# SSD decay mask and per-sequence operands: 128-column ScalarE pieces in place of wide VectorE and GpSimd instructions

## The chip, the cores and the metric

One core of one Trainium2 chip runs the kernel. The metric is the device time of one execution in microseconds (us).

## The reference, cut to what matters

The kernel is one inference step of a hybrid decoder layer for 1024 prompt tokens and 8 sample sequences of 8 tokens (1088 tokens): a modulated norm, one wide input projection, three groups of dilated attention, a Mamba-2 (SSD) branch, and an output projection. The change lies in the SSD branch. For one head the reference computes, with chunks of 128 tokens:

```python
# cs: cumulative sum of dt*A within a chunk; xdt = x * dt
L   = exp(cs_i - cs_j)  for i >= j, else 0          # decay inside a chunk
y  += (C_i . B_j) * L[i, j] * xdt_j                  # masked, chunk by chunk
state_c = state_(c-1) * exp(cs_end) + sum_j B_j * exp(cs_end - cs_j) * xdt_j
# sample tokens: state_b' = state_b * exp(cs_end_b) + sum over the 8 tokens of sequence b
```

The masked decay is made from relu(cs_j - cs_i), then exp of its negative, then a product with the causally masked C.B (`CB`). The states of the 8 sample sequences need, for each sequence b, the 64 sample rows multiplied by a 0/1 column that is 1 on the rows of b (`bmask`).

## The kernel before, in words

fp32 products are done on TensorE (PE) as three matmuls of a high and a low part: hi*hi, hi*lo, lo*hi (`mm3`, lines 196, 197, 198). Before a weight tile is used, ScalarE (ACT) rounds it to its high part `whi` (line 189) and VectorE (DVE) subtracts to get the low part `wlo` (line 190).

The stages follow each other: start to about 100 us, attention to about 780 us, SSD from about 780 to 1560 us, output projection to the end. In the SSD stage `run(jobs)` does projection jobs, each in three chunks of 368, 368 and 352 columns with 24 matmuls a chunk. A job's results leave PSUM (3 banks for these `pj` tiles) by an evacuation: of a conv job by ACT into `raw` (lines 858, 860), then a causal convolution of width 4 (ACT line 873, three times DVE line 875), a tanh (ACT line 877) and the products of lines 880 and 882 (DVE) that finish `xc`; of a z job by tanh (ACT line 891) and a product that reads the same bank again (DVE line 892), which frees the bank; of a gate job by ACT (`sg`, line 457).

Beside them runs a side generator: per head group of 4 tiles, `side()` transposes B, multiplies C.B into `CB`, and calls `x_tile` for the tiles xt = 4*gr to 4*gr+3, 16 in all, two heads each. The order of TensorE's queue is written out by hand: the generator yields, with a planned number of ns, and its matmuls are put between the k steps of the projection at that point. For every other engine a scheduler (the tile framework) decides the order of the instructions from the program; each engine then works its queue strictly in that order, and waits at the head of it.

What `x_tile` does, by lines of the kernel before:

- Line 973: a DMA on SyncE's (SP) queue broadcasts two rows of `cs` into `csb` (128 x 2 x 1088). `csb` has one buffer, so it starts after the last `yd` matmul of the tile before.
- Lines 977 and 980 (DVE): tok - csb, in one instruction of 128x2048 for the prompt and one of 128x128 for the sample. Then per head: relu (ACT line 983) and exp(-x) (ACT line 984), 128x1088 each, and the product with `CB` (DVE line 985).
- After the conv job of this tile is done (`xc`), PE transposes it to tokens (`tt`, line 209), DVE makes `xdt` (line 1003), GpSimd (POOL) `xde` (line 1008), DVE `xd` (line 1011), ACT its high part `xdh` (line 1013) and DVE the rest (line 1014). Line 1016, twice: POOL multiplies `xdh` and `xd`, repeated 8 times, by `bmask`, into `xdm` (128x1024 each).
- `stt` matmuls; ACT copies the first chunk into `sta` (line 1029), and DVE chains 14 steps over the other seven chunks (line 1033). `yo` matmuls read `sta` (14 of them, in two PSUM banks), then `ys` (ACT line 1044), `u` (DVE lines 1055, 1060), the `sts` matmuls that read `xdm`, and later the `yd` matmuls that read `csb`; then `u` is finished (line 1090), squared on ACT (lines 1093, 1096) and added into `sq` on POOL.

By what stands next to a tile in the program there are four kinds. In tiles 2, 6, 10 the conv of the same tile runs while `csb` is made. Tiles 1, 5, 9, 13 and tiles 3, 7, 11, 15 have a gate or other evacuation between. Tiles 0, 4, 8, 12 open a head group, and the conv of the next group's B is near.

Of the kernel before, what the change touches and what calls it, by code (L numbers as in the profile page):

```python
# [11 lines left out]
AF = mybir.ActivationFunctionType  # L12
OP = mybir.AluOpType
# [4 lines left out]
T = 1024  # L18
NB = 8
NS = 8  # L20
TS = NB * NS
TT = T + TS
# [4 lines left out]
CH = 128  # L27
# [82 lines left out]
def trunk(ctx: ExitStack, tc: tile.TileContext, I, O):  # L110
    nc = tc.nc
    V, S, G, PE, SP = nc.vector, nc.scalar, nc.gpsimd, nc.tensor, nc.sync
# [34 lines left out]
    def P(name):  # L147
        a, n = PACK[name]
        return pack[:, a:a + n]
# [228 lines left out]
    tok = const.tile([128, 9, 96], F32, name="tok")  # L378
# [448 lines left out]
    with ExitStack() as bctx:  # L827
# [98 lines left out]
        def side():  # L926
            for gr in range(4):
# [24 lines left out]
                for xt in range(4 * gr, 4 * gr + 4):  # L952
                    yield from x_tile(gr, xt, Bk, Bs, CB, CT, CS, sq)
                    order.passed.add(("x", xt))
# [15 lines left out]
        def x_tile(gr, xt, Bk, Bs, CB, CT, CS, sq):  # L970
            h0 = 2 * xt
            csb = b1.tile([128, 2, TT], F32, tag="csb", name="csb")
            SP.dma_start(out=csb, in_=bass.AP(tensor=cs_d.tensor, offset=cs_d[0, h0].offset,
                                              ap=[[0, 128], [TT, 2], [1, TT]]))
            mt = [csb[:, h, :] for h in range(2)]

            V.tensor_tensor(csb[:, :, :T].rearrange("p h (c l) -> p h c l", l=CH),  # L977
                            tok[:, :8, 32 + h0:34 + h0].rearrange("p c h -> p h c")[:, :, :, None].to_broadcast([128, 2, 8, CH]),
                            csb[:, :, :T].rearrange("p h (c l) -> p h c l", l=CH), op=OP.subtract)
            V.tensor_tensor(csb[:, :, T:], tok[:, 8, 32 + h0:34 + h0, None].to_broadcast([128, 2, TS]),  # L980
                            csb[:, :, T:], op=OP.subtract)
            for m in mt:
                S.activation(m, m, AF.Relu)
                S.activation(m, m, AF.Exp, scale=-1.0)
                V.tensor_mul(m, m, CB)  # L985
            ecs = b1.tile([128, TT], F32, tag="ecs", name="ecs")
# [26 lines left out]
            S.activation(xdh, xd, AF.Copy)  # L1013
            V.tensor_sub(xd, xd, xdh.bitcast(F32))
            for o, i in zip(xdm, (xdh.bitcast(F32), xd)):
                G.tensor_tensor(o, i[:, None, :].to_broadcast([128, NB, 128]),
                                P("bmask")[:, :, None].to_broadcast([128, NB, 128]), op=OP.mult)

            yield 6500.0,

# [1 line left out]
            for q in range(2):  # L1022
# [3 lines left out]
                for c in range(4):  # L1026
                    i = 4 * q + c
# [31 lines left out]
            for e in range(2):  # L1059
# [7 lines left out]
                            op=OP.mult)  # L1067
# [39 lines left out]
    with pool("yr", 2) as yr, pool("yw", 2) as yw:  # L1107
        def split(x, scale=1.0):
            hi = yp.tile([128, TT], F32R, tag="yh", name="yhi")
            lo = yp.tile([128, TT], F32R, tag="yh", name="ylo")  # L1110
            S.activation(hi, x, AF.Copy, scale=scale)
            if scale == 1.0:
                V.tensor_sub(lo, x, hi.bitcast(F32))
            else:
                V.scalar_tensor_tensor(lo, x, scale, hi.bitcast(F32), op0=OP.mult, op1=OP.subtract)
            return hi, lo
# [22 lines left out]
        for gr in range(5):  # L1139
# [9 lines left out]
            for m in range(8):  # L1149
# [25 lines left out]
                if gr == 4:  # L1175

                    a, b = split(acc[m], 0.5)
# [12 lines left out]
    for t in range(9):  # L1190
# [6 lines left out]
        m = 2 if t < 8 else 4  # L1197
        w = D // m
        for i in range(m):
            ps = bankA("fo")[:n, :w]  # L1200
            cs = slice(i * w, (i + 1) * w)
# [14 lines left out]
        for i in range(2):  # L1216
            cs = slice(i * 512, (i + 1) * 512)
# [152 lines left out]
```

## Time and profile before

| what | us |
|---|---|
| median of 3 runs | 1945.5 |
| lowest and highest run | 1937.53, 1951.32 |
| the profiled execution, its own time | 1937.77 |
| its span in the trace | 1935.9 |
| SSD stage in it | 780 to 1560 |

The span runs from the first to the last instruction of the trace. Everything below is read from this one execution. A row of a timeline or of a table of groups gives the busy time of an instruction; consecutive instructions of an engine overlap a little, so starts lie closer than the busy times. Numbers after an arrow name what ended an idle time.

### The profile page before, as it was taken

The page shows a single profiled execution, that of the slowest core. Times are in us where ns is not written, and L with a number is a line of the kernel's source. Part 1 is how long each engine was busy: PE and PEld are TensorE (multiplying, and loading weights), DVE is VectorE, ACT ScalarE, POOL GpSimd, SP SyncE. Part 2 cuts the span into 40 slices and gives each one's busy share as a digit, 9 for nine tenths or more (in the row PEclk, how much of TensorE's full clock was granted, in tenths as well). Part 3 has the DMA queues.
Part 4 walks back from the last instruction along what each step waited for, and adds up shares of the span by engine and source line. Part 5 has one row for each costly group of instructions (what it writes and reads, how often), then busy time and mean ns, then how long its engine had stood idle before and what let it go on. Part 6 is the DMA issues. An engine that isn't in the chain of part 4 may idle for free.

```text
span 1935.9 us, 31991 instructions
## 1 busy us (share of the span) xinstructions
PE 1873.6 (97%) x13065; PEld 1760.3 (91%) x13065; DVE 1062.1 (55%) x1974; ACT 644.9 (33%) x1260; POOL 327.7 (17%) x356
## 2 busy tenths in 40 slices
PE   5999999999999999999999999999999999999998
PEld 4989989988998998999999999999999899999987
DVE  5643243324324323577757775767679655466654
ACT  4443324313423432424342335233533331131222
POOL 2200010001002001132314221422142300000400
PEclk9999999999999999999999999999999999999999
DMA  8322462273256227434443543344233453364322
GB/s 338 121 69 102 132 223 69 87 221 132 96 156 195 83 89 238 148 124 164 148 136 114 169 159 124 117 155 138 81 99 121 153 188 117 127 200 148 123 87 76
DMA packets 108986, 269.54 MB, mean 139 GB/s; under 512 B 41600, under 2 KB 50632, under 8 KB 105576
## 3 DMA queue, kind: packets, MB, share of 16 engines
q1 hardware_dynamic: 108840, 267.51, 42.1%
q8 instruction: 102, 1.67, 0.4%
q14 instruction: 44, 0.36, 0.1%
HBM read 224.93 MB, written 80.26 MB: 158 GB/s over the span
## 4 chain that ended last, share of the span: by engine, by line
PE 50%; DVE 7%; DMA 6%; issue 3%; ACT 2%; POOL 0%; SPq 0%; ACTq 0%; DVEq 0%; POOLq 0%
PE pj L196 12%; PE pj L197 12%; PE pj L198 12%; DMA csb<-cs_d 3%; PE yd L205 2%; PE fo L1207 2%; PE fo L1205 2%; PE fo L1206 2%; PE yo L205 1%; DMA yx<-u_d 1%; DVE wlo L190 1%; DVE csb L977 1%; DVE csb L985 1%; PE sts L205 1%; PE stt L205 1%
## 5 line engine op out<-in xcount | busy, mean ns | idle before, releaser
L196 PE MATMUL pj<-h_hi,whi 128*128 128x368 f32 x2256 | 757.1, 336 | 5.2 <-DVE zs L892 4.7
L198 PE MATMUL pj<-h_lo,whi 128*128 128x368 f32 x2256 | 740.6, 328 | 0.0
L197 PE MATMUL pj<-h_hi,wlo 128*128 128x368 f32 x2256 | 740.1, 328 | 0.0
L196 PEld LDWEIGHTS pj<-h_hi,whi 128*128 128x128 f32 x2256 | 426.1, 189 | 30.9 <-issue 21.1
L197 PEld LDWEIGHTS pj<-h_hi,wlo 128*128 128x128 f32 x2256 | 426.3, 189 | 0.7
L198 PEld LDWEIGHTS pj<-h_lo,whi 128*128 128x128 f32 x2256 | 425.9, 189 | 0.0
L190 DVE TENSOR_TENSOR wlo<-wraw,whi 128x1024 fp32r<-128x1024 f32 (+1 forms) x136 | 163.5, 1202 | 247.8 <-ACT whi L189 245.5
L189 ACT ACTIVATE whi<-wraw 128x1024 fp32r<-128x1024 f32 (+1 forms) x136 | 126.6, 931 | 377.3 <-PE pj L198 369.9
L196 PE MATMUL pj<-yhi,whi 128*128 128x368 f32 (+1 forms) x480 | 157.5, 328 | 1.2 <-DVE acc L1169 1.1
L197 PE MATMUL pj<-yhi,wlo 128*128 128x368 f32 (+1 forms) x480 | 157.7, 328 | 0.2
L198 PE MATMUL pj<-ylo,whi 128*128 128x368 f32 (+1 forms) x480 | 157.1, 327 | 0.0
L626 ACT ACTIVATE pr<-pr,st 128x128 f32<-128x128 f32 (+1 forms) x192 | 83.9, 438 | 88.9 <-DVE st L623 88.7
L197 PEld LDWEIGHTS pj<-yhi,wlo 128*128 128x128 f32 x480 | 90.1, 188 | 3.0 <-issue 2.1
L196 PEld LDWEIGHTS pj<-yhi,whi 128*128 128x128 f32 x480 | 90.1, 188 | 3.0 <-ACT whi L189 1.4
L198 PEld LDWEIGHTS pj<-ylo,whi 128*128 128x128 f32 x480 | 90.1, 188 | 0.0
L875 DVE SCALAR_TENSOR_TENSOR xc<-raw,cw,xc 128x1112 f32<-128x1112 f32 x60 | 82.2, 1369 | 3.1 <-ACT xc L873 2.2
L645 DVE COPY pT<-pt 128x512 f32<-128x512 f32 x40 | 27.6, 689 | 102.3 <-ACT pT L647 40.4
L977 DVE TENSOR_TENSOR csb<-tok,csb 128x2048 f32<-128x2048 f32 x16 | 45.2, 2824 | 45.9 <-DMA csb<-cs_d 45.9
L1174 POOL TENSOR_TENSOR acc<-acc,ta 128x368 f32<-128x368 f32 (+1 forms) x24 | 24.2, 1010 | 263.8 <-DVE ta L1173 263.8
L506 DVE COPY k<-pj 128x368 f32<-128x368 f32 (+2 forms) x44 | 24.0, 581 | 81.3 <-PE pj L198 79.8
L858 ACT ACTIVATE raw<-pj 128x368 f32<-128x368 f32 (+1 forms) x72 | 31.9, 446 | 87.2 <-PE pj L198 84.5
L623 DVE CUSTOM_DVE_ANT_0 pr<-s,msk 128x128 f32<-128x128 f32 (+1 forms) x192 | 55.4, 346 | 7.8 <-PE s L205 7.5
(282 smaller groups left out, 2533.5 us busy)
## 6 DMA issues: line engine op xcount, KB each, us to landing
wraw<-in_w_in SPq DMA_DIRECT2D x96, 512.0 KB, 3.9
csb<-cs_d SPq DMA_DIRECT2D x16, 1088.0 KB, 6.5
kt<-in_kc SPq DMA_DIRECT2D x32, 448.0 KB, 4.6
out_kc<-in_kc SPq DMA_DIRECT2D x32, 448.0 KB, 4.7
out_vc<-in_vc SPq DMA_DIRECT2D x28, 512.0 KB, 5.1
vt<-in_vc SPq DMA_DIRECT2D x28, 512.0 KB, 5.9
sg_d<-sg SPq DMA_DIRECT2D x16, 544.0 KB, 3.0
ecs<-cs_d SPq DMA_DIRECT2D x32, 272.0 KB, 5.0
```

Source lines behind the costliest of these rows:

```text
L189: S.activation(hi, raw, AF.Copy)
L190: V.tensor_sub(lo, raw, hi.bitcast(F32))
L196: PE.matmul(ps, whi[:, k, :], xhi[k], start=first and k == 0, stop=False)
L197: PE.matmul(ps, wlo[:, k, :], xhi[k], start=False, stop=False)
L198: PE.matmul(ps, whi[:, k, :], xlo[k], start=False, stop=last and k == n - 1)
L205: PE.matmul(out, w, x, **kw)
L623: V.tensor_tensor_reduce(out=pr[:, h, c0:c0 + m], in0=ps[h][:, c0:c0 + m], in1=msk[:, h, w - m:w], scale=-1.0, scalar=3e38, op0=OP.add, op ...
L626: S.activation(pr[:, h, c0:c0 + m], pr[:, h, c0:c0 + m], AF.Exp, scale=-1.0, bias=st[:, 0, h, u:u + 1], accum_out=st[:, 1, h, u:u + 1])
L875: V.scalar_tensor_tensor(c, raw[:, t:t + CONV], cw[:, j, t:t + 1], c, op0=OP.mult, op1=OP.add)
L977: V.tensor_tensor(csb[:, :, :T].rearrange("p h (c l) -> p h c l", l=CH), tok[:, :8, 32 + h0:34 + h0].rearrange("p c h -> p h c")[:, :, :, ...
L1205: PE.matmul(ps, hi, whi[:, k, cs], start=k == 0, stop=False)
L1206: PE.matmul(ps, lo, whi[:, k, cs], start=False, stop=False)
```

## The change: pieces on ScalarE

Line 977, line 980 and the two wide relus go. In their place ACT makes, per head and chunk, relu(-1 * csb + tok column) with the column as the bias operand of the activation: 8 pieces of 128x128 and one of 128x64 per head, 18 per tile, at line 980 of the new program. The exp and the product with `CB` stay (lines 981 and 982 there). The two POOL instructions of line 1016 go too; in their place ACT makes 16 pieces of 128x128, a copy with the column of `bmask` as scale operand (line 1014 there). The row numbers of later lines drop by 3.

```diff
-            V.tensor_tensor(csb[:, :, :T].rearrange("p h (c l) -> p h c l", l=CH),
-                            tok[:, :8, 32 + h0:34 + h0].rearrange("p c h -> p h c")[:, :, :, None].to_broadcast([128, 2, 8, CH]),
-                            csb[:, :, :T].rearrange("p h (c l) -> p h c l", l=CH), op=OP.subtract)
-            V.tensor_tensor(csb[:, :, T:], tok[:, 8, 32 + h0:34 + h0, None].to_broadcast([128, 2, TS]),
-                            csb[:, :, T:], op=OP.subtract)
-            for m in mt:
-                S.activation(m, m, AF.Relu)
+            for h, m in enumerate(mt):
+
+                for c in range(9):
+                    cs = slice(c * 128, min(TT, c * 128 + 128))
+                    S.activation(m[:, cs], m[:, cs], AF.Relu, scale=-1.0, bias=tok[:, c, 32 + h0 + h:33 + h0 + h])
                 S.activation(m, m, AF.Exp, scale=-1.0)
                 V.tensor_mul(m, m, CB)
...
             for o, i in zip(xdm, (xdh.bitcast(F32), xd)):
-                G.tensor_tensor(o, i[:, None, :].to_broadcast([128, NB, 128]),
-                                P("bmask")[:, :, None].to_broadcast([128, NB, 128]), op=OP.mult)
+                for b in range(NB):
+                    S.activation(o[:, b, :], i, AF.Copy, scale=P("bmask")[:, b:b + 1])
```

The order of TensorE's queue stays. The scheduler's order on ACT and DVE moves. On ACT, at tile 6 (`raw` and `xc` belong to the conv of tile 6, `zs` to its z job, `s` to the end of tile 5), a row per run of like instructions, `-` before and `+` now:

```order
-L858 ACTIVATE raw<-pj 128x288
-L860 ACTIVATE raw<-pj 128x8x8
-L873 ACTIVATE xc<-raw,cb,cw 128x1112
-L983 ACTIVATE csb<-csb 128x1088 x2
-L891 ACTIVATE zs<-pj 128x368
-L984 ACTIVATE csb<-csb 128x1088 x2
-L891 ACTIVATE zs<-pj 128x368
-L877 ACTIVATE raw<-xc 128x1112
-L189 ACTIVATE whi<-wraw 128x1024
-L891 ACTIVATE zs<-pj 128x352
```

Before, `L873` stands right behind the evacuation of `raw`, ahead of the relus (983) and exps (984). On ACT at the same place, what stands there now, as far as the second exp (981):

```order
+L1093 ACTIVATE s_10269<-u 128x1088
+L980 ACTIVATE csb<-csb,tok 128x128 x7
+L189 ACTIVATE whi<-wraw 128x1024
+L980 ACTIVATE csb<-csb,tok 128x128
+L980 ACTIVATE csb<-csb,tok 128x64
+L980 ACTIVATE csb<-csb,tok 128x128 x8
+L980 ACTIVATE csb<-csb,tok 128x64
+L858 ACTIVATE raw<-pj 128x288
+L860 ACTIVATE raw<-pj 128x8x8
+L981 ACTIVATE csb<-csb 128x1088
+L891 ACTIVATE zs<-pj 128x368
+L981 ACTIVATE csb<-csb 128x1088
```

Now all 18 pieces stand ahead of the evacuation, and the rows that follow the last one shown are `L873`, `L891`, `L189`, `L891`, `L877`: the convolution's first step stands behind both exps, and its tanh behind the `whi` of a weight and the third `zs`.

On DVE at the same place, the rows from there on now:

```order
+L190 TENSOR_TENSOR wlo<-wraw,whi 128x1024
+L982 TENSOR_TENSOR csb<-csb,CB 128x1088
+L892 SCALAR_TENSOR_TENSOR zs<-zs,pj 128x368
+L982 TENSOR_TENSOR csb<-csb,CB 128x1088
+L875 SCALAR_TENSOR_TENSOR xc<-raw,cw,xc 128x1112
+L892 SCALAR_TENSOR_TENSOR zs<-zs,pj 128x368
+L875 SCALAR_TENSOR_TENSOR xc<-raw,cw,xc 128x1112
 L190 TENSOR_TENSOR wlo<-wraw,whi 128x1024
 L892 SCALAR_TENSOR_TENSOR zs<-zs,pj 128x352
```

Before, the order was 977, 980, wlo, two of 875, zs, the third 875, two of 985, zs, 880, 882, then a `wlo`. Now both products with `CB` stand ahead of the first 875, and a `wlo` and the third `zs` ahead of the third.

On ACT at tile 5, from `zs` of its z job to `sta` (`sg` is a gate's evacuation):

```order
+L1014 ACTIVATE xdm_9974<-xdh,pack 128x128 x3
+L980 ACTIVATE csb<-csb,tok 128x128 x8
+L980 ACTIVATE csb<-csb,tok 128x64
+L980 ACTIVATE csb<-csb,tok 128x128 x8
+L980 ACTIVATE csb<-csb,tok 128x64
+L1014 ACTIVATE xdm_9974<-xdh,pack 128x128 x4
+L981 ACTIVATE csb<-csb 128x1088
+L1014 ACTIVATE xdm_9974<-xdh,pack 128x128
+L1014 ACTIVATE xdm_9975<-xd,pack 128x128 x7
+L981 ACTIVATE csb<-csb 128x1088
+L1014 ACTIVATE xdm_9975<-xd,pack 128x128
+L457 ACTIVATE sg<-pj 128x368
```

The next row there is the copy into `sta` (L1026 now, L1029 before). Before, between that `zs` and that copy there stood two relus, the `sg` and one exp. Now all 34 pieces and both exps stand between.

## Rows read from the trace of the kernel before

**Rows 1.** Busy us (instructions) in the SSD stage: PE, PEld, DVE, ACT, POOL; clock, DMA.
```profile
780.00:1560.00 780.00, 761.10 (x5282) 734.18 (x5281) 553.06 (x845) 287.42 (x432) 228.62 (x200) 0.99 0.41 135
```
**Rows 2.** Waits of PE, 780 to 1560 us: what, us, times, longest.
```profile
PE pj L196 <- DVE zs L892: 4.7, 5, 2.5
PE yo L205 <- DVE sta L1033: 3.0, 4, 1.1
```
**Rows 3.** Groups of ACT by shape, whole span: count, busy us, mean ns.
```profile
L626 ACT ACTIVATE pr<-pr,st 128x128 f32<-128x128 f32 x104 | 40.6, 391 | 72.0 <-DVE st L623 72.0
...
L983 ACT ACTIVATE csb<-csb 128x1088 f32<-128x1088 f32 x32 | 33.8, 1106 | 67.0 <-DVE csb L980 67.0
```
**Rows 4.** Timeline of ACT in attention: start, busy us.
```profile
316.78 0.39 ACT L626 ACTIVATE pr<-pr,st 128x128 f32<-128x128 f32 x1
317.07 0.19 ACT L626 ACTIVATION_READ_ACCUMULATOR pr<-pr,st 128x1 f32 x1
```
**Rows 5.** Groups of DVE and POOL that go.
```profile
L977 DVE TENSOR_TENSOR csb<-tok,csb 128x2048 f32<-128x2048 f32 x16 | 45.2, 2824 | 45.9 <-DMA csb<-cs_d 45.9
...
L1016 POOL TENSOR_TENSOR xdm<-xd,pack 128x1024 fp32r<-128x1024 f32 x16 | 38.5, 2407 | 10.7 <-DVE xd L1014 10.7
```
**Rows 6.** Timeline at tile 6 (ACT, DVE).
```profile
1089.30 1.32 ACT L873 ACTIVATE xc<-raw,cb,cw 128x1112 f32<-128x1112 f32 x1
...
1097.37 1.14 ACT L877 ACTIVATE raw<-xc 128x1112 f32<-128x1112 f32 x1 [0.79 <-DVE xc L875]
1099.66 1.06 ACT L189 ACTIVATE whi<-wraw 128x1024 fp32r<-128x1024 f32 x1 [1.14 <-PE pj L198]
...
1089.20 2.29 DVE L977 TENSOR_TENSOR csb<-tok,csb 128x2048 f32<-128x2048 f32 x1 [4.87 <-DMA csb<-cs_d]
...
1092.77 2.78 DVE L875 SCALAR_TENSOR_TENSOR xc<-raw,cw,xc 128x1112 f32<-128x1112 f32 x2
...
1097.20 2.49 DVE L985 TENSOR_TENSOR csb<-csb,CB 128x1088 f32<-128x1088 f32 x2
1099.60 0.53 DVE L892 SCALAR_TENSOR_TENSOR zs<-zs,pj 128x368 f32<-128x368 f32 x1
...
1100.19 1.22 DVE L882 SCALAR_TENSOR_TENSOR xc<-raw,xc 128x1024 f32<-128x1024 f32 x1
...
1101.64 1.22 DVE L190 TENSOR_TENSOR wlo<-wraw,whi 128x1024 fp32r<-128x1024 f32 x1
```
**Rows 7.** Timeline of PE at tile 6.
```profile
1101.46 1.09 PE L209 MATMUL tt<-pack,xc 128*128 128x128 f32 x8 [0.83 <-DVE xc L882]
```
**Rows 8.** Timeline at tile 5 (ACT, DVE, PE).
```profile
1056.38 0.31 ACT L1013 ACTIVATE xdh<-xd 128x128 fp32r<-128x128 f32 x1 [1.63 <-DVE xd L1011]
1056.60 1.05 ACT L189 ACTIVATE whi<-wraw 128x1024 fp32r<-128x1024 f32 x1
1057.55 0.44 ACT L891 ACTIVATE zs<-pj 128x352 f32<-128x352 f32 x1
...
1066.24 0.26 ACT L1029 ACTIVATE sta<-stt 128x128 f32<-128x128 f32 x1
...
1069.16 2.38 DVE L1033 SCALAR_TENSOR_TENSOR sta<-sta,eall,stt 128x64 f32<-128x64 f32 x12
...
1069.64 2.07 PE L205 MATMUL yo<-CT,sta 128*128 128x128 f32 x14
```
**Rows 9.** Timeline at tile 7 (ACT, PE).
```profile
1138.22 0.48 ACT L457 ACTIVATE sg<-pj 128x368 f32<-128x368 f32 x1 [0.79 <-PE pj L198]
...
1146.10 0.26 ACT L1029 ACTIVATE sta<-stt 128x128 f32<-128x128 f32 x1
...
1151.36 0.87 PE L205 MATMUL yo<-CT,sta 128*128 128x128 f32 x4 [0.64 <-DVE sta L1033]
```
**Rows 10.** PE's gap at 1519 us, and the stretch behind it.
```profile
1519.41 0.47 PE L196 MATMUL pj<-h_hi,whi 128*128 128x352 f32 x1 [2.46 <-DVE zs L892]
...
1519.60:1523.00 3.40, 3.40 (x13) 3.40 (x13) 3.40 (x8) 1.76 (x4) 0.00 (x0) 0.51 0.51 154
```

## The prediction

> **What bounds the kernel now.** I read the busy time by stretch first, then what PE waits for, then the queues of ACT and DVE around those waits. In the SSD stage PE is busy for 761.1 of 780 us [rows 1], so it is the bound and can win back at most 18.9 us. ACT (287.4 us) and POOL (228.6 us) have much room by the average; DVE has 553.1. But the average is not the limit: each queue works in order, and PE's few waits are for short chains that run through ACT and DVE just before a fixed place of PE's own order. The reader is to see in the list of waits that the two largest that DVE sets, a bank that `zs` frees (4.7 us) and `yo` for the chain of `sta` (3.0 us), are only 7.7 us in all [rows 2], and that at tile 6 the transposes `tt` wait .83 us for `xc` [rows 7]. So `xc` and `sta` are nearly late already, with no slack to take more.
>
> **The price of a piece.** The nearest row is line 626: 128x128, fp32, with a bias column, 0.391 us [rows 3]; the instruction behind it starts 0.29 us later [rows 4]. No row shows a queue of pieces alone. Lower end: `xdh`, 128x128 with no column, after which the next starts 0.22 us later [rows 8]. Upper end: no overlap, 0.39. I take 0.29, and 0.24 for the 64 columns. So 18 pieces are 5.2 us a tile (16*0.29 + 2*0.24 = 5.1, and a first start), from 3.9 to 7.0; the 16 copies are 4.7, from 3.5 to 6.3. Two wide relus go, 1.106 us each [rows 3], about 1.0 apart. ACT gains 5.2 - 2.0 + 4.7 = 7.9 us a tile, 126 over 16 tiles: 413 of 780 us. Its total still fits.
>
> **What goes from DVE and POOL.** Line 977 took 2.82 us on the mean, 45.2 in all; POOL loses 32 instructions, those on `xd` with a mean of 2.41 [rows 5]. None of this is PE's time; it pays only where PE waits for DVE. Line 977 also stood at the head of DVE's queue until the `csb` DMA landed (45.9 us of waiting, rows 5). This wait now stands at the head of ACT's queue, and what is queued behind it there decides the rest. The DMA's own issue on SP, behind the last `yd`, does not move.
>
> On the price, a rule bears against the change: the Trainium skill ("ScalarE: Activation LUTs", Rules for kernel authors) has relu, add and mul done on VectorE, not ScalarE. By row, one DVE instruction of 2.29 us for 2048 columns [rows 6] is replaced by 16 pieces of 4.6 us, and the trace agrees as far as that goes; the sum is no other by it.
>
> **Tiles 2, 6, 10.** I follow tile 6. The DMA lands at 1089.2 (DVE's wait ends there, rows 6). Before, ACT did line 873 at 1089.30, and `tt` started at 1101.46 [rows 6, 7]; without its wait PE would have been there at 1100.6. Now ACT stands at the first piece until 1089.2, although it had nothing else to wait for. Seven pieces to 1091.25, a `whi` (0.95) to 1092.2, eleven pieces to 1095.3, two evacuations (0.45) to 1095.75, exp, `zs`, exp to 1098.1, then line 873: 8.8 us later than before. On DVE the products with `CB` (1.25 each, rows 6) come ahead of the convolution: first step at 1099.85 (1.37 each by rows 6), `zs` (0.45), second to 1102.95, `wlo` (1.2), `zs` (0.45), third to 1105.95. ACT's tanh (1.14) takes it to 1107.1, lines 880 and 882 (1.4) to 1108.5. So `tt` starts about 1108.55, 7.1 us later than before, and PE waits nearly 8 us in place of 0.83.
>
> PE's own clock: at 1519 us it stood for 2.46 us, and the 3.4 us behind that ran at a granted clock of 0.51 [rows 10], the lower of its two levels, so 1.7 us of work were lost. I add 1.7 for each of these long waits. Per tile 8.8, three tiles: 26.4 us. Even if pieces cost nothing, `whi` after PE's last matmul at 1099.66 [rows 6], then `wlo`, `zs`, the third step, tanh and 882 make `tt` late by 4.8 each.
>
> **Tiles 1, 5, 9, 13.** Tile 5: after `zs` at 1057.55 [rows 8] ACT works three copies, all 18 pieces, four copies, exp, eight copies, exp, one copy, `sg`, then the copy into `sta`: 1057.9 + 0.9 + 5.2 + 1.2 + 1.0 + 2.3 + 1.0 + 0.3 + 0.35, so 1070.15 in place of 1066.24 [rows 8], 3.9 later. DVE's 14 steps (12 took 2.38, so 0.2 each, rows 8) then start at about 1070.85 behind the last product with `CB`, in place of ending near 1071.5. The last `yo` ends near 1074.0 in place of 1071.7 [rows 8]. That is +2.3, with what PE wins at `zs` already inside. Tile 9, whose DMA was late before, +1.1. Sum 3*2.3 + 1.1 = 8.0 us.
>
> **Tiles 3, 7, 11, 15.** Tile 7: the gate's `sg` stood free at 1138.22; it now stands behind all pieces, copies and exps, near 1150.3, and PE wants its bank at about 1148.5 (some 2 us of wait). `sta` moves from 1146.10 to 1150.5, and `yo` ends at 1155.0 in place of 1152.2 [rows 9]: +2.7, three times. Tile 15 wins: its gap of 2.46 us and the slow stretch behind it [rows 10] go, and the later `sta` takes most back, -1.1. Sum 7.0 us.
>
> **Tiles 0, 4, 8, 12, and 14.** The conv of B stands behind 13 pieces, but its transposes come later; tile 8, whose DMA took longer, +1.4; tile 0 +0.4; the others 0. Sum 1.8 us.
>
> **The sum** is 26.4 + 8.0 + 7.0 + 1.8 = 43.2 us. Against the profiled execution's own 1937.8 us this gives 1981. That execution lies 7.7 us under the median of the runs, 1945.5, from which it would be 1988.7. I forecast 1985, between them.
>
> **Rivals.**
> First, faster. DVE's queue is no longer held by the DMA and 2.8 us of work, and POOL no longer slows it: then `zs`, `sta` and the gap at 1519 vanish, 4.7 + 3.0 us, plus 1.7 of clock, so 9.4 us less: 1928 from the profiled execution, 1936 from the median. For it: the same kind of instruction on DVE took 2.29 us alone [rows 6] and 2.82 on the mean [rows 5]. The Trainium skill ("GPSIMD Engine Reference", its specification table) says that GpSimd shares its SBUF interfaces with VectorE and names instructions with two SBUF inputs; by that rule DVE's whole work beside line 1016 shrinks. Against it: the place is ACT's queue ahead of line 873 and of `sta`. The price is 5.2 us of pieces plus the wait for the DMA; it would decide only if `csb` landed some 9 us sooner at tiles 2, 6, 10, which its issue behind `yd` excludes. Chance 0.04.
>
> Second, no change beyond noise. With pieces at 0.22 us, tiles 1, 3 and their like come out even (some 34 pieces stand ahead of `sta`, and 34*0.07 is 2.4 us less), and tiles 2, 6, 10 keep their 4.8 to 5.5 us: 15 to 17 us, 1953 to 1962. What is measurable here is about 1% of 1945.5, 19.5 us. Chance 0.08.
>
> Third, much worse. Pieces at 0.39 us add 0.1 * 34 = 3.4 us to the chain of each of the 11 tiles counted, 35 us, and a lowered clock after the waits of tiles 1 and 3 and their like adds up to 7 * 1.7 = 12: in all 75 to 90 us, 2013 to 2035. For it: no row shows pieces that read and write the same buffer in a row. Against it: the spacing of 0.29 [rows 4] is a like instruction's. Chance 0.14.
>
> The forecast's own case has 0.74. Within it, 0.26 to 0.33 us a piece and no or one lowered clock a tile give 30 to 60 us. The range of eight in ten takes in half of the second and third: 1960 to 2020. From the cases: faster by over 1% 0.03 (the first rival mostly ends within 1%), within 1% 0.10, slower 0.87.
>
> **What would show it.** Right: PE's waits in the SSD stage are headed by `tt` for `xc`, 7 to 8 us, three times, with a granted clock near 0.5 behind them; then `yo` for `sta`; ACT near 413 us of the stage, DVE near 490; a piece's busy time near 0.39 and spacing near 0.29; line 873 at tiles 2, 6, 10 some 9 us after `csb` lands. Wrong: if PE's idle time in the stage is under 30 us, or if `tt` waits under 4 us at those tiles, my walk of ACT's queue fails; if it is over 80 us, a piece costs more than I took, or a bank's evacuation behind the pieces stops the projection at more places than tiles 3, 7, 11.

## The result, and the profile after

The changed kernel took 1987.96 us (median of 4 runs, 1985.61 to 1993.19), the kernel before, beside it and over 4 runs, 1944.09: a ratio of 1.0249, interval [1.0214, 1.0283], so 2.5% slower. The forecast was 1985. The profiled execution took 1987.65 us with a span of 1985.9, 50.0 longer than that of before. The medians lie 43.9 us apart: the profiled execution of before was one of its fastest (1937.77 us). What follows explains the 50.0 us between one execution of each.

Busy time of each engine in the whole span, from the page of the changed kernel, part 1:

```profile
PE 1893.4 (95%) x13065; PEld 1775.9 (89%) x13065; DVE 995.9 (50%) x1942; ACT 767.4 (39%) x1772; POOL 253.2 (13%) x324
```

The SSD stage of the changed kernel (busy us and instructions of PE, PEld, DVE, ACT, POOL, then the granted clock), to set against [rows 1]:

```profile
780.00:1610.00 830.00, 779.97 (x5289) 748.40 (x5289) 487.51 (x813) 409.86 (x944) 153.96 (x168) 0.97 0.39 127
```

ACT took on 122 us and still idles half the stage; DVE and POOL lost 66 and 75. PE is idle for 830.00 - 779.97 = 50.0 us in place of 18.9, so 31.1 us more. For nearly the same number of matmuls (5289 and 5282) it is also busy 18.9 us longer, and most of that is its clock. These are the sums over the stretches of the stage in which the lower level was granted, eleven in the changed kernel and then four in the kernel before (their length, then the busy times in them):

```profile
sum 58.01, PE 46.61 PEld 43.91 DVE 40.58 ACT 15.50 POOL 8.27; mean PE 4.24 PEld 3.99 DVE 3.69 ACT 1.41 POOL 0.75
sum 17.05, PE 17.05 PEld 16.99 DVE 15.06 ACT 7.12 POOL 0.00; mean PE 4.26 PEld 4.25 DVE 3.76 ACT 1.78 POOL 0.00
```

Counting half of PE's busy time as lost at a granted clock of 0.50, that is 23.3 us now and 8.5 before, so 14.8 us more. The other 4.1 us of busy time include the seven matmuls more and are not taken apart. The changed kernel also enters the stage 1.5 us late: from 770.5 us on, ahead of the first piece, its clock was at the lower level for 3.4 us, and that of before was not.

What PE waits for in the stage now (us, times, longest), against [rows 2]:

```profile
PE tt L209 <- DVE xc L882: 22.1, 3, 7.4
PE yo L205 <- ACT sta L1026: 8.5, 5, 2.1
PE pj L196 <- ACT sg L457: 5.9, 3, 2.1
PE yo L205 <- DVE sta L1030: 4.9, 9, 1.4
...
PE pj L196 <- ACT raw L860: 1.7, 3, 0.8
```

The waits for the `zs` banks are gone from the list. In their place stand three long waits for `xc`, 13.4 us for `sta`, 5.9 for the banks of the gates, and 1.7, at tiles 2, 6 and 10, for the bank of `raw`, whose evacuation stands behind the pieces. The longest of them lead back to ACT's queue. At tile 6, ACT and then PE of the changed kernel (start, busy us):

```profile
1112.95 2.16 ACT L980 ACTIVATE csb<-csb,tok 128x128 f32<-128x128 f32 x7 [4.18 <-DMA csb<-cs_d]
1115.02 1.05 ACT L189 ACTIVATE whi<-wraw 128x1024 fp32r<-128x1024 f32 x1
1115.97 3.21 ACT L980 ACTIVATE csb<-csb,tok 128x128 f32<-128x128 f32 x11
...
1121.84 1.31 ACT L873 ACTIVATE xc<-raw,cb,cw 128x1112 f32<-128x1112 f32 x1
...
1129.55 1.13 ACT L877 ACTIVATE raw<-xc 128x1112 f32<-128x1112 f32 x1 [4.40 <-DVE xc L875]
```
```profile
1132.12 1.75 PE L209 MATMUL tt<-pack,xc 128*128 128x128 f32 x7 [7.41 <-DVE xc L882]
```

ACT stands 4.18 us before the first piece, until the DMA of `csb` lands. Line 873 starts 8.9 us after that; in the kernel before it started 0.1 us after the landing [rows 6]. PE then stands 7.41 us where it stood 0.83 [rows 7].

### The profile page after: what moved, and what is told of

It reads as the page before. It is cut to its first block, busy times and chain, and to the rows that moved or that the text cites. A ratio compares the mean times of both kernels' runs of the same rounds, so it can differ in the third digit from the quotient of the medians.

```text
span 1985.9 us, 32395 instructions
## 1 busy us (share of the span) xinstructions
PE 1893.4 (95%) x13065; PEld 1775.9 (89%) x13065; DVE 995.9 (50%) x1942; ACT 767.4 (39%) x1772; POOL 253.2 (13%) x324
## 4 chain that ended last, share of the span: by engine, by line
PE 50%; ACT 8%; DMA 5%; DVE 5%; issue 1%; POOL 0%; ACTq 0%; DVEq 0%; POOLq 0%
PE pj L196 12%; PE pj L197 12%; PE pj L198 12%; DMA csb<-cs_d 3%; ACT csb L980 3%; ACT xdm L1014 2%; PE yd L205 2%; PE fo L1204 2%; PE fo L1203 2%; PE fo L1202 2%; PE yo L205 2%; ACT csb L981 1%; PE sts L205 1%; PE tt L209 1%; DVE wlo L190 1%
## 5 line engine op out<-in xcount | busy, mean ns | idle before, releaser
L190 DVE TENSOR_TENSOR wlo<-wraw,whi 128x1024 fp32r<-128x1024 f32 (+1 forms) x136 | 157.3, 1157 | 289.7 <-ACT whi L189 287.5
L189 ACT ACTIVATE whi<-wraw 128x1024 fp32r<-128x1024 f32 (+1 forms) x136 | 126.4, 931 | 363.2 <-PE pj L198 347.7
L980 ACT ACTIVATE csb<-csb,tok 128x128 f32<-128x128 f32 (+1 forms) x288 | 85.1, 382 | 27.3 <-DMA csb<-cs_d 27.3
L982 DVE TENSOR_TENSOR csb<-csb,CB 128x1088 f32<-128x1088 f32 x32 | 42.5, 1338 | 75.9 <-ACT csb L981 75.9
L1030 DVE SCALAR_TENSOR_TENSOR sta<-sta,eall,stt 128x64 f32<-128x64 f32 x224 | 45.1, 274 | 36.0 <-ACT sta L1026 36.0
```

What stands on the lines that cost most here:

```text
L189: S.activation(hi, raw, AF.Copy)
L190: V.tensor_sub(lo, raw, hi.bitcast(F32))
L980: S.activation(m[:, cs], m[:, cs], AF.Relu, scale=-1.0, bias=tok[:, c, 32 + h0 + h:33 + h0 + h])
L1030: V.scalar_tensor_tensor(sta[:, i, hs], sta[:, i - 1, hs], eall[:, h0 + h, i:i + 1], ps[:, c, hs], op0=OP.mult, op1=OP.add)
```

## The experiments

Two theories were set against each other. By the place theory the pieces cost PE time only where something urgent stands behind them in ACT's queue: the convolution (line 873) at tiles 2, 6, 10, the copy into `sta` and the gates' evacuations at tiles 1, 3 and their like. By the volume theory the time follows the ScalarE time added. Ratios are to the kernel before, run beside each. Run e7 is not in the table: it leaves out the decay of all chunks but the first, and it was run once (1932.14 us, against 1940.84 for the kernel before).

| run | ratio | interval |
|---|---|---|
| the change | 1.0249 | 1.0214 to 1.0283 |
| e1, exponents only | 1.0073 | 1.0052 to 1.0095 |
| e2, bmask products only | 1.0032 | 1.0011 to 1.0053 |
| e3, exponents, held until sta | 1.0035 | 1.0014 to 1.0055 |
| e4, as e3, and bmask products | 1.0112 | 1.0074 to 1.0149 |
| e5, exponents, held until xc | 0.9907 | 0.9883 to 0.9930 |
| e6, as e5, and bmask products | 1.0099 | 1.0076 to 1.0122 |
| e8, the change with 34 half pieces | 1.0430 | 1.0396 to 1.0464 |
| e9, the change, sta copy on VectorE | 1.0112 | 1.0079 to 1.0144 |
| e10, as e6, sta copy on VectorE | 0.9963 | 0.9949 to 0.9977 |

### The two parts alone (e1, e2)

e1 keeps the two GpSimd instructions of line 1016, e2 keeps the wide VectorE subtraction and the relus (of each, one line of the change):

```diff
 # e1: of the change only
+                    S.activation(m[:, cs], m[:, cs], AF.Relu, scale=-1.0, bias=tok[:, c, 32 + h0 + h:33 + h0 + h])
 # e2: of the change only
+                    S.activation(o[:, b, :], i, AF.Copy, scale=P("bmask")[:, b:b + 1])
```

> Only the decay exponents on ScalarE; the bmask products stay on GpSimd. Place theory (what counts is what stands behind the pieces at the head of ScalarE's queue): the long waits of the transposes for xc at tiles 2, 6, 10 stay as in the changed kernel, 6 to 8 us each, some 25 us with the clock; tiles 1, 3 and their like come out at or a little under the kernel before, since 18 pieces take about as long as the relus and the wait for VectorE did. In all 15 to 30 us slower than before. Volume theory (the time follows the ScalarE time added, 3.2 of 7.9 us a tile): about 18 us, spread over all 16 tiles.

> Only the bmask products as 16 ScalarE copies; the wide VectorE subtraction and relus stay. Place theory: the copies run between xdh and the wait for VectorE, nothing urgent stands behind them, no long wait at tiles 2, 6, 10: within 8 us of the kernel before, and VectorE's line 977 shorter than its mean of 2.82 us. Volume theory: 4.7 of 7.9 us a tile, about 26 us slower.

PE's waits in e1, and then in e2 with the group of line 977:

```profile
PE tt L209 <- DVE xc L882: 22.6, 4, 7.4
...
PE yo L205 <- DVE sta L1031: 0.2, 1, 0.2
```
```profile
PE yo L205 <- DVE sta L1033: 9.4, 10, 1.1
...
PE tt L209 <- DVE xc L882: 3.7, 3, 1.6
```
```profile
L977 DVE TENSOR_TENSOR csb<-tok,csb 128x2048 f32<-128x2048 f32 x16 | 36.6, 2290 | 40.8 <-DMA csb<-cs_d 40.8
```

In e1 the long waits for `xc` are all there, and those for `sta` are gone: the exponents alone make tiles 2, 6, 10 late and the others a little early (medians 1954.67 against 1938.28, 16.4 us). The time of e1 alone would fit both theories (15 to 30 us, and 18); the three waits fit the place theory. In e2 the copies cost 7 us, not 26, so there the time does not follow the ScalarE time. Both expectations of the place theory held in size, but e2 showed something that I had not named, at tile 7 (DVE, then ACT):

```profile
1148.12 2.03 DVE L980 TENSOR_TENSOR csb<-tok,csb 128x128 f32<-128x128 f32 x1
1150.07 0.28 DVE L1014 TENSOR_TENSOR xd<-xd,xdh 128x128 f32<-128x128 f32 x1
```
```profile
1152.20 2.44 ACT L1017 ACTIVATE xdm<-xd,pack 128x128 fp32r<-128x128 f32 x8
1154.54 0.25 ACT L1029 ACTIVATE sta<-stt 128x128 f32<-128x128 f32 x1
```

The rest `xd` stands on DVE behind `csb`; so eight of the copies come late and sit just ahead of `sta`. The second thing to see is line 977 itself: 2.29 us on the mean without the GpSimd products, 2.82 with them [rows 5]. In the kernel before, the eight executions of line 977 that no product of line 1016 overlaps took 2.29 to 2.34 us, the eight that one overlaps 2.53 to 3.98. So the products did slow VectorE. The Trainium skill ("GPSIMD Engine Reference", specification table) names this contention, for VectorE instructions with two SBUF inputs, and the trace agrees: line 977 reads `tok` and `csb`. The gain is 8.6 us of DVE's time; PE's time shows none of it, for e2 is slower.

The parts do not add: 0.7% and 0.3% alone, 2.5% together. e1 has almost no wait for `sta` (0.2 us), the change has 13.4: the exponents alone fit in front of `sta`, both sets do not.

### The pieces held back (e3, e4)

A small VectorE instruction copies the 18 bias columns after the first chunk of `sta`, and the pieces read the copy; the pieces, the exps and the products with `CB` are written behind `ys` (these moved lines are left out here). e4 has the bmask copies on ScalarE too.

```diff
+                        V.scalar_tensor_tensor(tb, sta[:, 0, :18].rearrange("p (h c) -> p h c", h=2), 0.0,
+                                               tok[:, :, 32 + h0:34 + h0].rearrange("p c h -> p h c"), op0=OP.mult, op1=OP.add)
```

> Exponents on ScalarE, but their bias columns are copied through a small VectorE instruction that reads the first chunk of sta, so that no piece can stand ahead of the convolution or of the copy into sta; bmask products on GpSimd. Place theory: no long wait for xc, and the waits for the zs banks and sta shrink: 8 us faster to 6 us slower than the kernel before. Volume theory: some 18 us slower, as with the pieces in their place. What could go wrong for both: csb is late for yd (at tiles 5 and 7 about 12 us lie between sta and yd, and the pieces, exps and one product need about 9).

> As the run before, with the bmask products as ScalarE copies too: the whole change with its pieces held back. Place theory: within 12 us of the kernel before. Volume theory: 40 us or more slower, as the changed kernel.

Both came out slower than the place theory had said: 7.9 and 23 us. PE's largest wait in e3, the wait at tile 7 there, and the largest of e4:

```profile
PE tt L209 <- DVE xc L882: 17.6, 8, 2.9
```
```profile
1136.20 1.97 PE L209 MATMUL tt<-pack,xc 128*128 128x128 f32 x8 [2.92 <-DVE xc L882]
```
```profile
PE tt L209 <- DVE xc L882: 29.5, 9, 4.7
```

The waits moved. Held until `sta`, the pieces fall into the convolution of the next tile (ahead of tile 7, line 873 starts at 1122.02 us behind all 18 of them and both exps), and `xc` is late at eight tiles by up to 2.9 us in place of three by 7.4. My expectation had looked at what stands behind `csb` in its own tile only. The two runs support the place theory as to the mechanism, not in its numbers.

### Held until the tile's own convolution (e5, e6)

The bias columns are copied when `xc` is done, ahead of `xdt`, so the pieces can stand neither ahead of the convolution of this tile nor in that of the next. Their lines, the exps and the products with `CB` are written behind it (left out here).

```diff
+            V.scalar_tensor_tensor(tb, xc[:, :18].rearrange("p (h c) -> p h c", h=2), 0.0,
+                                   tok[:, :, 32 + h0:34 + h0].rearrange("p c h -> p h c"), op0=OP.mult, op1=OP.add)
```

> Exponents on ScalarE with bias columns that a small VectorE instruction copies once the tile's own convolution is done (it reads 18 columns of xc); bmask products on GpSimd. The pieces then can stand neither ahead of line 873 of their own tile nor, as with the columns held back until sta, ahead of that of the next one. Place theory: the three long waits of run e1 (about 28 us of its trace with the clock) go and its gains at tiles 1, 3 and their like stay: 4 to 14 us faster than the kernel before, 1924 to 1934. Volume theory: about 18 us slower, as ScalarE does the same work as in e1.

> The same with the bmask products as ScalarE copies too. Place theory: tiles 2, 6, 10 without their long waits, but at tiles 1, 3 and their like 34 pieces still stand ahead of the copy into sta: 10 to 25 us slower than the kernel before. Volume theory: 40 us or more.

PE's waits in e5, without those for `ms` (3.9 us) and `cb` (3.0), which are in every kernel at about this size; then PE's busy time from 780 to 1540 us in e5, and in the kernel before:

```profile
PE tt L209 <- DVE xc L882: 0.7, 1, 0.7
PE pj L196 <- DVE acc L1170: 0.6, 1, 0.6
PE yo L205 <- DVE sta L1034: 0.5, 2, 0.3
PE pj L196 <- DVE zs L892: 0.2, 1, 0.2
```
```profile
780.00:1540.00 760.00, 751.74 (x5245) 728.13 (x5244) 511.90 (x828) 334.61 (x685) 234.11 (x200) 0.99 0.41 138
```
```profile
780.00:1540.00 760.00, 741.99 (x5162) 715.46 (x5161) 545.68 (x832) 279.60 (x421) 226.11 (x199) 0.99 0.41 132
```

e5 has the 18 pieces a tile of e1 and 55 us more ScalarE time than before in this stretch, and is 0.9% faster than the kernel before: 1921.37 against 1940.84. It is the best version found. PE is idle 8.3 us where it was idle 18.0, and gets 83 more matmuls done. The gain, 19.5 us, is more than the 4 to 14 that I had expected. e6 adds the bmask copies and loses 1.9%; its largest waits:

```profile
PE yo L205 <- DVE sta L1033: 9.6, 11, 1.5
PE yo L205 <- ACT sta L1029: 7.9, 5, 1.9
```

No wait for `xc` is in its list; what it has beyond e5's list are these for `sta` and 0.8 us for the gates' banks.

### The price of a piece (e7, e8)

```diff
 # e7, with line 1016 as before
+                S.activation(m, m, AF.Relu, scale=-1.0, bias=tok[:, 0, 32 + h0 + h:33 + h0 + h])
 # e8, in the changed kernel
-                for c in range(9):
-                    cs = slice(c * 128, min(TT, c * 128 + 128))
+                for c in range(17):
+                    cs = slice(c * 64, c * 64 + 64)
 ...
```

> As e1, but the 9 pieces of a head are one instruction of 1088 columns with the column of the first chunk as bias for all, so the decay of the other chunks is left out of the computation; the order at tiles 2, 6, 10 stays (line 873 behind both exps). It takes the price of the pieces away (2.0 in place of 5.2 us a tile) and leaves their place. Place theory: the waits of tt for xc stay at 4 to 5.5 us each. Were the price of the pieces the cause, they would fall to 1 us or less, as in the kernel before.

> The changed kernel with its exponents in 34 pieces of 64 columns a tile in place of 18. At an estimated 0.24 us each, 8.2 in place of 5.2 us a tile. If a piece's time counts at each of the 11 tiles where they stand ahead of xc or sta: some 3 us each, 25 to 40 us slower than the changed kernel. If the wait for the DMA alone counted: no change.

e7's wait for `xc`, and the group of the half pieces of e8 with its four largest waits:

```profile
PE tt L209 <- DVE xc L882: 10.8, 3, 3.6
```
```profile
L980 ACT ACTIVATE csb<-csb,tok 128x64 f32<-128x64 f32 x544 | 134.4, 334 | 30.0 <-DMA csb<-cs_d 30.0
```
```profile
PE yo L205 <- ACT sta L1026: 18.3, 4, 5.2
PE pj L196 <- ACT sg L457: 15.5, 4, 5.4
PE tt L209 <- DVE xc L882: 13.6, 5, 3.4
PE pj L196 <- ACT raw L860: 12.4, 3, 4.1
```

e7 lies between the two expectations: with the pieces' time gone the three waits are 3.6 us, a little under the 4 to 5.5, and far from the 0.83 of before. So of the 7.4 us about half is what the place costs with any relu there. The other half is mostly the price of the pieces: at tile 6 of e7 line 873 starts 5.6 us after the landing, 3.3 sooner than in the changed kernel. Up to 0.9 us of it is another order: line 882 follows 8.1 us behind line 873 in place of 9.0, since the third 875 there stands ahead of a `wlo` and a `zs`.

e8 is 1.0430 against 1.0249, some 35 us more. That is the total expected, 3 us at each of 11 tiles, but it did not arise at all of them. Between the same matmuls of the two traces, the half pieces add 2.0, 4.9, 4.1 and 3.4 us at tiles 1, 5, 9, 13, and 3.5, 3.5 and 3.8 at tiles 3, 7, 11: there the price passes to PE. At tiles 2, 6, 10 they add only 0.3, 0.9 and 0.6. At tile 6 PE now stands 4.10 us for the bank of `raw` and then 3.26 for `xc`, in place of 0.53 and 7.41; line 873 starts 12.2 us after the landing in place of 8.9, but `tt` follows it in 8.4 us in place of 10.3. So at these tiles a longer queue of pieces need not lengthen PE's wait, and the total was met in part by luck.

### The copy into sta taken out of ScalarE's queue (e9, e10)

```diff
-                        S.activation(sta[:, 0, :], ps[:, 0, :], AF.Copy)
+                        V.tensor_copy(sta[:, 0, :], ps[:, 0, :])
```

> The changed kernel, with the first copy into sta made by VectorE instead of ScalarE, so that no piece stands ahead of it. Place theory: PE's waits for sta (13.4 us in the changed kernel) go and the gates' banks are still late; the three long waits for xc stay: 10 to 22 us faster than the changed kernel, some 25 to 35 us slower than the kernel before. Volume theory: as the changed kernel within 5 us, since ScalarE does the same work but for one copy of 0.26 us a tile.

> Run e6 (all pieces on ScalarE, exponents held back until the tile's convolution is done) with the copy into sta on VectorE too. Now neither xc nor sta stands behind a piece. Place theory: the 17.5 us of waits for sta in e6 and the clock behind them go: 10 us faster to 4 us slower than the kernel before, although all 34 pieces a tile are on ScalarE. Volume theory: as e6, 15 to 20 us slower than before.

The largest waits of e9, then of e10, and e10's stage in the same columns as before:

```profile
PE tt L209 <- DVE xc L882: 21.9, 3, 7.4
PE pj L196 <- ACT sg L457: 6.0, 3, 2.2
```
```profile
PE pj L196 <- ACT sg L457: 6.2, 3, 2.4
```
```profile
780.00:1610.00 830.00, 815.37 (x5646) 790.46 (x5645) 528.59 (x886) 419.99 (x948) 152.91 (x165) 0.99 0.43 138
```

e9 has the changed kernel's waits but those for `sta`; by the spans of the two profiled executions, 1967.7 and 1985.9, it is 18.2 us faster than the changed kernel, by the ratios 1.0112 and 1.0249 some 26, a little more than the 10 to 22 expected; it is 23.8 us slower than the kernel before, where 25 to 35 had been expected. e10 has every piece of the change on ScalarE, 420 us of its time in the stage, and is 0.4% faster than the kernel before. With that the volume theory falls: the same pieces on the same engine make the kernel 2.5% slower or 0.4% faster by where they stand and what stands behind them (e10 also has the copy into `sta`, 0.26 us a tile, on VectorE).

## Why the prediction was right, step by step

The difference between the starts of the same matmul in the two traces, taken at the borders of the tiles, gives each step's share. The last two columns are PE's idle time added, and half of the busy time added at the lower clock; a small part is in neither.

| tiles | forecast, us | measured, us | idle | clock |
|---|---|---|---|---|
| 2, 6, 10 | 26.4 | 9.6 + 9.1 + 9.5 = 28.2 | 21.0 | 6.6 |
| 1, 5, 9, 13 | 8.0 | 5.2 + 2.5 + 1.8 + 3.4 = 12.9 | 5.6 | 6.5 |
| 3, 7, 11, 15 | 7.0 | 2.9 + 2.9 + 3.1 + 0.7 = 9.6 | 5.1 | 3.4 |
| the rest | 1.8 | -0.7 | -2.5 | 0.7 |
| sum | 43.2 | 50.0 | 29.2 | 17.2 |

The columns of the rest run over the whole span, from the first matmul to the last. Their small sums hide larger parts: 1.7 us lost ahead of the stage (at 770 us), 1.7 lost behind tile 3 and again behind tile 15, and 5.1 won behind tiles 7 and 11, where only the kernel before fell to the lower clock.

- **The price of a piece** was right. Groups of ACT by shape (count, busy us, mean ns), and 18 pieces in a row at tile 7:

```profile
L980 ACT ACTIVATE csb<-csb,tok 128x128 f32<-128x128 f32 x256 | 78.8, 388 | 27.3 <-DMA csb<-cs_d 27.3
L1014 ACT ACTIVATE xdm<-xdh,pack 128x128 fp32r<-128x128 f32 x128 | 40.3, 390 | 0.2
```
```profile
1170.51 5.27 ACT L980 ACTIVATE csb<-csb,tok 128x128 f32<-128x128 f32 x18 [0.70 <-DMA csb<-cs_d]
```

  The forecast was 0.39 us of busy time and 5.2 us for 18, from a like instruction of another stage [rows 3, 4].

- **Tiles 2, 6, 10**: forecast line 873 some 9 us after the DMA lands (8.9 measured) and 7 to 8 us of wait (7.4). The walk of the queue held instruction by instruction. The 4.8 us that it gave to the place alone did not: in e7 `tt` waits 3.6 us, some 2.7 longer than before, with one step of the convolution placed otherwise. The second rival rested on that term.

- **Tiles 3, 7, 11**: `sg` at tile 7 was forecast to stop PE for some 2 us. ACT, then PE, at tile 7 of the changed kernel:

```profile
1182.38 0.46 ACT L457 ACTIVATE sg<-pj 128x368 f32<-128x368 f32 x1
1182.73 0.26 ACT L1026 ACTIVATE sta<-stt 128x128 f32<-128x128 f32 x1
```
```profile
1182.88 0.43 PE L196 MATMUL pj<-h_hi,whi 128*128 128x368 f32 x1 [1.91 <-ACT sg L457]
```

- **Tiles 1, 5, 9, 13**: too small, 8.0 for 12.9, and the reason is the clock: the added waits were smaller than forecast, 5.6 us, and 6.5 came on top at the lower level. Tile 5 came out as forecast (2.5 for 2.3). Tile 1, at which `sta` was late too, cost 5.2: PE's first `yo` there, and the granted clock behind it (the third figure from the end):

```profile
882.74 0.49 PE L205 MATMUL yo<-CT,sta 128*128 128x128 f32 x2 [2.15 <-ACT sta L1026]
...
883.20:890.00 6.80, 6.21 (x23) 5.51 (x23) 5.63 (x20) 0.11 (x1) 0.00 (x0) 0.50 0.04 12
```

  The lower clock level behind the waits at tiles 1, 3 and their like was in my third rival, as up to 12 us, and not in the sum; 9.9 us were measured. (That rival's other term was added up wrongly: 3.4 us at 11 tiles are 37.4, not 35.)

- **The split of the sum** was off, and the total hid it. The forecast was 39.8 us of added waits and 3.4 of clock (three falls at 1.7 less the one won at tile 15). Measured in the stage are 31.1 of waits and 14.8 of clock. Two errors, 8.7 us too much and 11.4 too little, nearly cancel, and that is luck. The step that failed is the price of a wait in clock: I took 1.7 us, from the one fall at 1519 us [rows 10], and only behind the waits at tiles 2, 6, 10. There it was of the right size at tile 6, and larger at tile 2, where the clock stayed at 0.50 behind the wait:

```profile
925.00:931.00 6.00, 5.62 (x21) 5.62 (x22) 4.38 (x7) 0.72 (x3) 2.60 (x4) 0.50 0.02 2
```

  The added waits came out 9 us smaller than forecast. At tiles 2, 6, 10 they were right, 21.0 for 21.3: those for `xc` are 22.1 us, of which 2.7 were there before, and the 1.7 for the bank of `raw` come on top. Too large were the terms of the other tiles: 5.6 measured for 8.0 at tiles 1, 5, 9, 13, and 5.1 for 8.7 (7.0 and the 1.7 of clock won) at tiles 3, 7, 11, 15.

- **The first rival** (faster, 9.4 us) named a real gain: `zs` waits gone, `sta` earlier, and the gap at 1519 us gone. e5 shows it at twice that size by the medians (19.5 us) once nothing urgent stands behind the pieces. The part on GpSimd is not in it: e5 keeps the products of line 1016 there. Its condition, though, was put wrongly: I wrote that it needs `csb` some 9 us sooner. It needs the pieces later, which the program can have with one small instruction. The second rival (within 1%) and the third (pieces 0.39 us apart) did not come about.

## What to carry to other kernels

Moving work to an engine with free time is priced by the queue, not by the share of busy time: find what stands right behind the moved instructions and ahead of whose wait it ends, and add the wait for their own input to their price. Where a scheduler pulls such work forward because it is ready early, a dependency on the right earlier result can hold it back; too late a one moves the wait to the next tile, as e3 and e4 show. And a wait of PE has a second price, the time at the lower clock behind it, here 14.8 us on top of 31.1 of waits.

## What the runs showed of the hardware that I had not expected

How PE's clock answers a wait. At tile 3 and at tile 7 PE stood for nearly the same time, for a gate's bank, in the same place of the program. The wait and the stretch behind it (the granted clock is the third figure from the end), at tile 3 and then at tile 7:

```profile
977.03 0.44 PE L196 MATMUL pj<-h_hi,whi 128*128 128x368 f32 x1 [1.93 <-ACT sg L457]
...
978.00:984.00 6.00, 4.59 (x30) 4.14 (x30) 5.80 (x18) 1.06 (x2) 0.00 (x0) 1.00 0.78 262
```
```profile
1183.60:1187.00 3.40, 3.40 (x15) 3.10 (x14) 3.40 (x13) 1.31 (x3) 0.00 (x0) 0.50 0.40 152
```

Behind the 1.93 us the clock stayed at its upper level, behind the 1.91 us it fell to the lower. So a wait of this size may cost its clock or not, and a forecast has to carry both. The same holds for `sta` at tiles 5 and 13: PE stood 1.39 us at each, and the clock fell behind the second alone. Even the short waits for `ms`, which are in every kernel, did it now and then: of the four in the stage (0.9 to 1.3 us), the clock fell behind three in the kernel before and behind two in the changed one. In sum the lower clock made some 15 of the 50.0 us.

And the way in which GpSimd slowed VectorE's line 977, which I had expected only on the mean (2.29 us without its products, 2.82 with them): half of the 16 executions in the kernel before were hardly touched, and one, which such products overlap from its start to its end, took 3.98.
